# Splitting the 512-column matmuls of the weight-stationary units into matmuls of 256 columns

## The chip, the core and the metric

The kernel runs on one NeuronCore of a Trainium2 chip. The metric is the device time of one execution in microseconds (us), from before the first instruction to after the last. A profiled execution also gives the span from the first instruction to the last, and what each engine did in it: TensorE (PE in the profile, and PEld for its weight loads), VectorE (DVE), ScalarE (ACT), GpSimd (POOL), SyncE (SP) and the DMA queues.

## What is computed

One encoder layer on 256 positions of width 2048, in fp32. Cut to its matrix products, the reference is:

```python
h = rmsnorm(x, norm1_gain)
proj = h @ w_in                      # 2048 x 6144
o_d, o_l = diff_attention(...), dilated_window(...)     # on the columns of proj
x = x + concat([o_d, o_l]) @ w_out   # 2048 x 2048
h2 = rmsnorm(x, norm2_gain)
g, u = split(h2 @ w_gate_up)         # 2048 x 11264
g = depthwise_conv(g, conv_w, conv_b)
x = x + (silu(g) * u) @ w_down       # 5632 x 2048
return rmsnorm(x, final_gain)
```

## The kernel before, in words

**Products in three parts.** Each fp32 operand is split into a high part in the type fp32r and a low part that is the rest (`split`, L118: ScalarE writes the high part, VectorE subtracts to get the low part). A product then is high by high, plus high by low, plus low by high; low by low is left out. Activations lie as `hT`, `h2T`, `mT`, `aT`, each `[128, k tile, 2, 256]`: for each block of 128 rows of the contraction the 256 tokens' high parts (call them ah), and right behind them the 256 low parts (al). Weights come as raw tiles of 1 MB by DMA; each raw tile is split into two units of 1024 columns, `whi` and `wlo`.

**Units.** The list `units` (L157 to L190) is the order of all the work. A unit is 1024 weight columns, 512 KB, and `products` (L212) issues its matmuls; `mm` (L210) is the helper, so nearly all matmuls have line L210. There are two forms:

- Form A, with stationary activations: V columns, output projection, down projection. A unit is 12 matmuls of 512 columns, whose moving operand is a slice of `whi` or `wlo`.
- Form B, with stationary weights: query and key columns (`qk`, 16 groups of 4 units, on `hT`), and gate and up columns (`g` and `u`, 22 pairs of 256 columns each, 4 units each, on `h2T`). That is 64 and 176 units, 240 in all. A unit holds 4 k tiles by 256 output columns, that is 8 stationary tiles of 128x128 of each of `whi` and `wlo`. The 256 output columns are two column blocks, c = 0 and c = 1, each with a PSUM bank of its own: the accumulator `acc` is `[128, 2, 512]`.

In form B before, the first pass runs over the 8 `whi` tiles, and each multiplies all 512 columns of a k tile, ah and al at once. High by high so lands in the first 256 columns of the bank, high by low in the second 256. The second pass runs over the 8 `wlo` tiles with ah alone, 256 columns, into the first half:

```python
if p == 0:
    mm(P[:, c], w, a[:, kt], U["first"] and i == 0, False)
else:
    mm(P[:, c, :S], w, a[:, kt, 0], False, U["last"] and i == nk - 1)
```

**Reading an accumulator.** After the fourth unit of a group the two halves of each bank are added up (`sum_parts`, L337): ScalarE copies the second halves to SBUF (`half`, L340), VectorE adds them to the first (L341). `evac_qk` (L343) then scales the key block by the row of 1/rms (`R1`, L347), `gate` (L573) scales by `R2` (L578) and goes into the convolution, and `gated` (L598) multiplies by the activated gate (L603) and splits the result into `aT`. There are two accumulators, so that one is summed while the next group fills the other.

**Order around the change.** The loop at L675 goes unit by unit: it issues the DMA of raw tiles some units ahead on SyncE's queue, splits the weights of the unit three ahead (`AHEAD = 3`), issues the matmuls of this unit, and then whatever is tied to this unit's end (the dictionary `post`): attention steps, evacuations, gating. Each engine runs its instructions in that order. In the `qk` part the attention's small matmuls (scores L364 to L367, transposes L400 and L465, attention times V L421 to L425; tiles named `at`) stand between units.

Of the kernel before, what the change touches and what calls it, by code (L numbers as in the profile page):

```python
# [9 lines left out]
F32 = mybir.dt.float32  # L10
F32R = mybir.dt.float32r
BF16 = mybir.dt.bfloat16
AF = mybir.ActivationFunctionType
# [3 lines left out]
S = 256  # L17
# [32 lines left out]
def encoder_layer(ctx, tc, xT_d, x_d, w_d, sm_d, tab_d, fg_d, id_d, oh_d, lnc_d, out_d):  # L50
    nc = tc.nc
# [7 lines left out]
    att = att_stack.enter_context(tc.tile_pool(name="att", bufs=2))  # L59
    ctx.enter_context(tc.manual_schedule())  # L60

    def at_tile():
        return pat.tile([128, 512], F32, name="at", tag="at")
# [40 lines left out]
    p = at_tile()  # L104
# [13 lines left out]
    def split(hi, lo, src, gain=None):  # L118

        if gain is None:  # L120
            nc.scalar.activation(hi, src, AF.Copy)  # L121
            nc.vector.tensor_sub(lo, src, hi.bitcast(F32))  # L122
        else:
            nc.scalar.activation(hi, src, AF.Copy, scale=gain)  # L124
            nc.vector.scalar_tensor_tensor(lo, src, gain, hi.bitcast(F32),
                                           op0=ALU.mult, op1=ALU.subtract)
# [82 lines left out]
    def mm(out, lhsT, rhs, start, stop):  # L209
        nc.tensor.matmul(out, lhsT, rhs, start=start, stop=stop)  # L210

    def products(s, ts=(0, 1)):  # L212
        U = units[s]
        if U["first"]:
            if U["key"] == ("d", 3):
                accs[U["key"]] = [at_tile(), at_tile()]
            else:
                P = acc.tile([128, 2, 512], F32, name="acc", tag="acc")
                accs[U["key"]] = P if U["form"] == "B" else [P[:, 0], P[:, 1]]
        P = accs[U["key"]]  # L220
        a = A[U["act"]]()
        hi, lo = W[s]
        nk = len(U["kts"])
        if U["form"] == "A":
            wh, wl = (w.rearrange("p (k c) -> p k c", k=2) for w in (hi, lo))
            seq = []
            for i, t in ((i, t) for i in range(2) for t in ts):
                seq += [(i, t, 0, 0), (i, t, 0, 1), (i, t, 1, 0)]
            for t in ts:
                mine = [x for x in seq if x[1] == t]  # L230
                firsts, lasts = mine[0], mine[-1]
                seq = [x + ((x == firsts), (x == lasts)) if x[1] == t else x for x in seq]
            for i, t, x_, w_, f_, l_ in seq:
                mm(P[t], a[:, U["kts"][i], x_, t * 128:(t + 1) * 128], (wh, wl)[w_][:, i],
                   U["first"] and f_, U["last"] and l_)
        else:
            wh, wl = (w.rearrange("p (k c) -> p k c", k=4) for w in (hi, lo))

            seq = [(i, c, p) for p in range(2) for i in range(nk) for c in range(2)]
            for i, c, p in seq:  # L240
                kt = U["kts"][i]
                w = (wh, wl)[p][:, i, c * 128:(c + 1) * 128]

                if p == 0:
                    mm(P[:, c], w, a[:, kt], U["first"] and i == 0, False)
                else:
                    mm(P[:, c, :S], w, a[:, kt, 0], False, U["last"] and i == nk - 1)


    Z = dram.tile([NH, 128, 512], F32, name="Z")  # L250
# [19 lines left out]
    cst = {}  # L270
# [63 lines left out]

    G = defaultdict(dict)

    def sum_parts(pool, out, P):  # L337

        h = pool.tile([128, 2, S], F32, name="half", bufs=1)
        nc.scalar.activation(h, P[:, :, S:], AF.Copy)  # L340
        nc.vector.tensor_add(out, P[:, :, :S], h)  # L341

    def evac_qk(g):  # L343
        P = accs.pop(("qk", g))
        qk = att.tile([128, 2, S], F32, name="qk", bufs=1)
        sum_parts(att, qk, P)
        nc.vector.tensor_mul(qk[:, 1], qk[:, 1], cst["R1"])  # L347
        G[g]["qk"] = qk

    def split_qk(g):  # L350
# [140 lines left out]
    for g in range(16):  # L491
        e = end_slot["qk", g]
        first(e, evac_qk, g)
        first(e + 1, split_qk, g)
        at_slot(e + SC, scores, g)
        off = [SC, TR, AV, NO, MX]
        if g < 8:
            if g % 2 == 0:
                continue
            at_slot(e + SC + 1, diff_mix, g)  # L500
            e += 1
            for k in range(2, 5):
                off[k] += DD
        at_slot(e + TR, transp, g)
        for k, f in ((2, av), (3, norm_o), (4, mix_out)):
            at_slot(e + off[k], f, g)
# [52 lines left out]
    ml = {}  # L559
# [13 lines left out]
    def gate(pr):  # L573
        P = accs.pop(("g", pr))
        pool = ml["pool"]
        G2 = ml["gs"]
        sum_parts(pool, G2[:, :, 1:S + 1], P)
        nc.vector.tensor_mul(G2[:, :, 1:S + 1], G2[:, :, 1:S + 1],  # L578
                             cst["R2"][:, None, :].to_broadcast([128, 2, S]))
        y = pool.tile([128, 2, S], F32, name="y", bufs=1)  # L580
        ml["y"] = y
        for c in range(2):
            f = 2 * pr + c
            w = [sm[:, C_CW + 3 * f + i:C_CW + 3 * f + i + 1] for i in range(3)]
            gs = G2[:, c]
            nc.scalar.activation(y[:, c], gs[:, 1:S + 1], AF.Identity, bias=sm[:, C_CB + f:C_CB + f + 1],
                                 scale=w[1])
            nc.vector.scalar_tensor_tensor(y[:, c], gs[:, 0:S], w[0], y[:, c], op0=ALU.mult, op1=ALU.add)
            nc.vector.scalar_tensor_tensor(y[:, c], gs[:, 2:S + 2], w[2], y[:, c],
                                           op0=ALU.mult, op1=ALU.add)  # L590
# [7 lines left out]
    def gated(pr):  # L598
        P = accs.pop(("u", pr))
        aT = ml["aT"]  # L600
        a = ml["pool"].tile([128, 2, S], F32, name="a", bufs=1)
        sum_parts(ml["pool"], a, P)
        nc.vector.tensor_mul(a, a, ml.pop(("s", pr)))  # L603
        f = 2 * pr
        split(aT[:, f:f + 2, 0], aT[:, f:f + 2, 1], a)

    for pr in range(FT // 2):
        at_slot(end_slot["g", pr], gate, pr)
        at_slot(end_slot["g", pr] + 1, silu, pr)
        at_slot(end_slot["u", pr], gated, pr)  # L610
# [64 lines left out]
    for s in range(-AHEAD, NU):  # L675
        while n_loaded < NU // 2 and n_loaded * 2 <= s + AHEAD + 4:
            for _ in load_raw(n_loaded, 2 if n_loaded < 5 else 1):
                pass
            n_loaded += 1
            if X0 <= n_loaded < X0 + 4:  # L680
                load_x(n_loaded - X0)
        v = s + AHEAD
        if v < 8:
            split_unit(v, 2, lambda i: split_x(2 * v + i))
        elif v < NU:
            split_unit(v)
        if s == NU - AHEAD:
            break
        if s >= 0:
            products(s)  # L690
            del W[s]
            for f, a in post.pop(s, ()):
                f(*a)
    assert not post

    for t in range(2):
        for u in range(s, NU):
            products(u, (t,))
        final(t)
# [96 lines left out]
```

## Time and profile before

| what | value |
|---|---|
| device time, median of 3 runs | 1139.54 us (1139.11 to 1141.63) |
| device time of the profiled execution | 1139.58 us |
| its span | 1137.6 us |
| outside the span | 2.0 us |
| TensorE busy | 1125.6 us, 99% of the span, 6004 matmuls |
| weight loads busy | 962.0 us, 85%, 6004 loads |
| VectorE busy | 714.7 us, 63% |
| ScalarE busy | 577.7 us, 51% |
| DMA | 219.63 MB, mean 193 GB/s |

The busy time of TensorE is from the start of a matmul to its modelled end, and matmuls overlap; what a matmul costs in a dense stretch is the distance from its start to the start of the next one. A weight load overlaps the matmul before it. The time outside the span is the profiled execution's device time less its span.

### The profile page before, as it was taken

The page shows a single profiled execution, that of the slowest core. Times are in us where ns is not written, and L with a number is a line of the kernel's source. Part 1 is how long each engine was busy: PE and PEld are TensorE (multiplying, and loading weights), DVE is VectorE, ACT ScalarE, POOL GpSimd, SP SyncE. Part 2 cuts the span into 40 slices and gives each one's busy share as a digit, 9 for nine tenths or more (in the row PEclk, how much of TensorE's full clock was granted, in tenths as well). Part 3 has the DMA queues.
Part 4 walks back from the last instruction along what each step waited for, and adds up shares of the span by engine and source line. Part 5 has one row for each costly group of instructions (what it writes and reads, how often), then busy time and mean ns, then how long its engine had stood idle before and what let it go on. Part 6 is the DMA issues. An engine that isn't in the chain of part 4 may idle for free.

```text
span 1137.6 us, 14934 instructions
## 1 busy us (share of the span) xinstructions
PE 1125.6 (99%) x6004; PEld 962.0 (85%) x6004; DVE 714.7 (63%) x901; ACT 577.7 (51%) x814; POOL 22.0 (2%) x40
## 2 busy tenths in 40 slices
PE   8999999999999999999999999999999999999996
PEld 6878888888888888888888888888888888888885
DVE  7845667766655576676676667667666645454543
ACT  7544455666655555455454545545454434343432
POOL 0000000000000000000000000000000000000000
PEclk9999999999999999999999999999999999999999
DMA  9578445544444545454545455463645655555551
GB/s 333 195 256 321 161 179 179 182 163 167 173 160 177 190 183 191 179 192 179 222 153 218 181 188 187 184 221 149 222 173 198 228 205 197 185 190 196 204 186 74
DMA packets 34078, 219.63 MB, mean 193 GB/s; under 512 B 3905, under 2 KB 4289, under 8 KB 9433
## 3 DMA queue, kind: packets, MB, share of 16 engines
q1 hardware_dynamic: 31536, 211.17, 51.1%
q0 software_dynamic: 1776, 6.69, 1.6%
q8 instruction: 47, 0.77, 0.3%
q10 hardware_dynamic: 696, 0.81, 0.2%
q14 instruction: 23, 0.18, 0.0%
HBM read 216.54 MB, written 5.27 MB: 195 GB/s over the span
## 4 chain that ended last, share of the span: by engine, by line
PE 98%; DMA 0%; issue 0%; ACT 0%; DVE 0%; POOLq 0%; POOL 0%; DVEq 0%
PE acc L210 90%; PE at L210 7%; PE at L400 0%; DMA sm<-sm 0%; PE at L531 0%; PE at L465 0%; ACT jk L645 0%; POOLq L792 0%; PE at L255 0%; POOL r L651 0%; PE at L150 0%; DVEq L792 0%; ACT hT L124 0%; DVE x L657 0%; DVE x L643 0%
## 5 line engine op out<-in xcount | busy, mean ns | idle before, releaser
L122 DVE TENSOR_TENSOR wlo<-raw,whi 128x1024 fp32r<-128x1024 f32 (+1 forms) x400 | 471.4, 1200 | 220.6 <-ACT whi L121 220.4
L121 ACT ACTIVATE whi<-raw 128x1024 fp32r<-128x1024 f32 (+1 forms) x400 | 408.3, 1036 | 218.4 <-PE acc L210 176.0
L210 PE MATMUL acc<-h2T,whi 128*128 128x512 f32 x1408 | 356.5, 395 | 0.0
L210 PEld LDWEIGHTS acc<-h2T,whi 128*128 128x128 f32 x1408 | 251.7, 188 | 47.0
L210 PEld LDWEIGHTS acc<-h2T,wlo 128*128 128x128 f32 x1408 | 186.7, 188 | 16.0
L210 PE MATMUL acc<-h2T,wlo 128*128 128x256 f32 x1408 | 189.1, 277 | 0.0
L210 PE MATMUL acc<-whi,aT 128*128 128x512 f32 x528 | 162.8, 389 | 0.0
L210 PE MATMUL acc<-hT,whi 128*128 128x512 f32 x512 | 131.2, 398 | 0.0
L210 PEld LDWEIGHTS acc<-whi,aT 128*128 128x128 f32 x528 | 99.1, 188 | 20.7
L210 PEld LDWEIGHTS acc<-hT,whi 128*128 128x128 f32 x512 | 91.5, 188 | 17.5
L210 PE MATMUL acc<-wlo,aT 128*128 128x512 f32 x264 | 102.7, 389 | 0.0
L340 ACT ACTIVATE half<-acc 128x512 f32<-128x512 f32 x60 | 35.6, 593 | 118.2 <-PE acc L210 118.2
L210 PE MATMUL acc<-whi,hT 128*128 128x512 f32 x256 | 82.1, 399 | 1.9 <-ACT hT L124 1.9
L210 PE MATMUL acc<-whi,mT 128*128 128x512 f32 x256 | 82.7, 395 | 0.0
L210 PEld LDWEIGHTS acc<-hT,wlo 128*128 128x128 f32 x512 | 68.1, 188 | 5.9
L210 PE MATMUL acc<-hT,wlo 128*128 128x256 f32 x512 | 69.0, 277 | 0.0
L210 PEld LDWEIGHTS acc<-whi,hT 128*128 128x128 f32 x256 | 48.8, 191 | 14.2 <-ACT hT L124 2.8
L210 PEld LDWEIGHTS acc<-wlo,aT 128*128 128x128 f32 x264 | 49.6, 188 | 10.1
L210 PEld LDWEIGHTS acc<-whi,mT 128*128 128x128 f32 x256 | 48.1, 188 | 9.7
L210 PE MATMUL at<-whi,aT 128*128 128x512 f32 x176 | 54.4, 389 | 0.0
L210 PE MATMUL acc<-wlo,hT 128*128 128x512 f32 x128 | 50.5, 394 | 0.0
L210 PE MATMUL acc<-wlo,mT 128*128 128x512 f32 x128 | 49.9, 390 | 0.0
(123 smaller groups left out, 677.5 us busy)
## 6 DMA issues: line engine op xcount, KB each, us to landing
raw<-w SPq DMA_DIRECT2D x191, 1024.0 KB, 4.8
raw<-w SPq DMA_DIRECT2D x8, 512.0 KB, 7.5
Z<-Td POOLq DMA_DIRECT2D x1, 3072.0 KB, 19.6
Xb<-Z POOLq DMA_DIRECT2D x12, 192.0 KB, 4.2
x<-x SPq DMA_DIRECT2D x4, 512.0 KB, 11.6
xT<-xT SPq DMA_DIRECT2D x7, 256.0 KB, 7.1
raw<-w SPq DMA_DIRECT2D x4, 256.0 KB, 5.4
fg<-fg POOLq DMA_DIRECT2D x1, 1024.0 KB, 5.1
```

The costliest lines, as they stand in the source:

```text
L121: nc.scalar.activation(hi, src, AF.Copy)
L122: nc.vector.tensor_sub(lo, src, hi.bitcast(F32))
L210: nc.tensor.matmul(out, lhsT, rhs, start=start, stop=stop)
L340: nc.scalar.activation(h, P[:, :, S:], AF.Copy)
```

## The change

Form A keeps its matmuls and their order; its code is only written more simply. In form B a unit is now one matmul of 512 columns (the first `whi` tile of column block 0, with ah and al) and 22 of 256 columns: the other 7 `whi` tiles with ah, then the same 7 with al, then the 8 `wlo` tiles with ah. All 22 add into the first half of their bank. So each of those 7 `whi` tiles is stationary twice, in two passes. The columns that are multiplied stay the same: 8 x 512 + 8 x 256 = 6144 before, 512 + 22 x 256 = 6144 now. The second half of a bank is written for column block 0 alone, and so the halves are added up for that block alone (`sum_first`); block 1 is read from PSUM by the multiplication that follows.

```diff
@@ products, form B
-            seq = [(i, c, p) for p in range(2) for i in range(nk) for c in range(2)]
-            for i, c, p in seq:
-                kt = U["kts"][i]
-                w = (wh, wl)[p][:, i, c * 128:(c + 1) * 128]
-
-                if p == 0:
-                    mm(P[:, c], w, a[:, kt], U["first"] and i == 0, False)
-                else:
-                    mm(P[:, c, :S], w, a[:, kt, 0], False, U["last"] and i == nk - 1)
+            parts = ((wh, 0), (wh, 1), (wl, 0))
+            mm(P[:, 0], wh[:, 0, :128], a[:, U["kts"][0]], U["first"], False)
+            seq = [(i, c, j) for j in range(3) for i in range(nk) for c in range(2)]
+            seq = [x for x in seq if x not in ((0, 0, 0), (0, 0, 1))]
+            for i, c, j in seq:
+                w, x_ = parts[j]
+                mm(P[:, c, :S], w[:, i, c * 128:(c + 1) * 128], a[:, U["kts"][i], x_],
+                   U["first"] and (i, c, j) == (0, 1, 0), U["last"] and j == 2 and i == nk - 1)
@@
-    def sum_parts(pool, out, P):
-        h = pool.tile([128, 2, S], F32, name="half", bufs=1)
-        nc.scalar.activation(h, P[:, :, S:], AF.Copy)
-        nc.vector.tensor_add(out, P[:, :, :S], h)
+    def sum_first(pool, out, P):
+        h = pool.tile([128, S], F32, name="half", bufs=1)
+        nc.scalar.activation(h, P[:, 0, S:], AF.Copy)
+        nc.vector.tensor_add(out, P[:, 0, :S], h)
@@ evac_qk
-        sum_parts(att, qk, P)
-        nc.vector.tensor_mul(qk[:, 1], qk[:, 1], cst["R1"])
+        sum_first(att, qk[:, 0], P)
+        nc.vector.tensor_mul(qk[:, 1], P[:, 1, :S], cst["R1"])
@@ gate
-        sum_parts(pool, G2[:, :, 1:S + 1], P)
-        nc.vector.tensor_mul(G2[:, :, 1:S + 1], G2[:, :, 1:S + 1],
-                             cst["R2"][:, None, :].to_broadcast([128, 2, S]))
+        sum_first(pool, G2[:, 0, 1:S + 1], P)
+        nc.vector.tensor_mul(G2[:, 1, 1:S + 1], P[:, 1, :S], cst["R2"])
+        nc.vector.tensor_mul(G2[:, 0, 1:S + 1], G2[:, 0, 1:S + 1], cst["R2"])
@@ gated
-        sum_parts(ml["pool"], a, P)
-        nc.vector.tensor_mul(a, a, ml.pop(("s", pr)))
+        s = ml.pop(("s", pr))
+        sum_first(ml["pool"], a[:, 0], P)
+        nc.vector.tensor_mul(a[:, 1], P[:, 1, :S], s[:, 1])
+        nc.vector.tensor_mul(a[:, 0], a[:, 0], s[:, 0])
```

On TensorE, at the end of a group of `qk` units with the scores of an earlier group behind it, the order before is (each row is a matmul, its result, what it reads, its columns, and how many stand in a row):

```order
L210 MATMUL acc<-hT,whi 128x512 x8
L210 MATMUL acc<-hT,wlo 128x256 x8
L210 MATMUL at<-qks 128x256 x6
L210 MATMUL acc<-hT,whi 128x512 x8
L210 MATMUL acc<-hT,wlo 128x256 x8
```

and at the same place now:

```order
L210 MATMUL acc<-hT,whi 128x512
L210 MATMUL acc<-hT,whi 128x256 x14
L210 MATMUL acc<-hT,wlo 128x256 x8
L210 MATMUL at<-qks 128x256 x6
L210 MATMUL acc<-hT,whi 128x512
L210 MATMUL acc<-hT,whi 128x256 x14
```

Eight matmuls of 512 columns became one of 512 and fourteen of 256; what stands around them is where it was. The units on `h2T` read the same way.

On VectorE, at the first pair of the gate and up columns, from the reading of the gate accumulator (`gs`) to that of the up accumulator (`a`), the order before is:

```order
L341 TENSOR_TENSOR gs<-acc,half 128x2x256
L578 TENSOR_TENSOR gs<-gs,R_3803 128x2x256
L588 SCALAR_TENSOR_TENSOR y<-gs,sm,y 128x256
L589 SCALAR_TENSOR_TENSOR y<-gs,sm,y 128x256
L588 SCALAR_TENSOR_TENSOR y<-gs,sm,y 128x256
L589 SCALAR_TENSOR_TENSOR y<-gs,sm,y 128x256
L122 TENSOR_TENSOR wlo<-raw,whi 128x1024
L595 TENSOR_TENSOR y<-y,R_3803 128x512
L122 TENSOR_TENSOR wlo<-raw,whi 128x1024 x3
L341 TENSOR_TENSOR a<-acc,half 128x512
L603 TENSOR_TENSOR a<-a,y 128x512
```

and now:

```order
L339 TENSOR_TENSOR gs<-acc,half 128x256
L576 TENSOR_TENSOR gs<-acc,R_4279 128x256
L577 TENSOR_TENSOR gs<-gs,R_4279 128x256
L586 SCALAR_TENSOR_TENSOR y<-gs,sm,y 128x256
L587 SCALAR_TENSOR_TENSOR y<-gs,sm,y 128x256
L586 SCALAR_TENSOR_TENSOR y<-gs,sm,y 128x256
L587 SCALAR_TENSOR_TENSOR y<-gs,sm,y 128x256
L122 TENSOR_TENSOR wlo<-raw,whi 128x1024
L593 TENSOR_TENSOR y<-y,R_4279 128x512
L122 TENSOR_TENSOR wlo<-raw,whi 128x1024 x3
L339 TENSOR_TENSOR a<-acc,half 128x256
L602 TENSOR_TENSOR a<-acc,y 128x256
```

Two operations on 512 columns became three on 256 at each reading; nothing else changed its place.

## Rows read from the trace of the kernel before

**Rows 1.** The page: span, busy time by engine, granted clock in 40 slices, chain by engine.

```profile
span 1137.6 us, 14934 instructions
PE 1125.6 (99%) x6004; PEld 962.0 (85%) x6004; DVE 714.7 (63%) x901; ACT 577.7 (51%) x814; POOL 22.0 (2%) x40
PEclk9999999999999999999999999999999999999999
PE 98%; DMA 0%; issue 0%; ACT 0%; DVE 0%; POOLq 0%; POOL 0%; DVEq 0%
```

**Rows 2.** Waits of TensorE in the whole span: us in total, times, longest.

```profile
PE acc L210 <- ACT hT L124: 1.9, 1, 1.9
PE at L106 <- DVE warm L67: 1.2, 1, 1.2
```

**Rows 3.** Groups by form, TensorE: count | busy us, mean ns of one | idle before.

```profile
L210 PE MATMUL acc<-h2T,whi 128*128 128x512 f32 x1408 | 356.5, 395 | 0.0
L210 PEld LDWEIGHTS acc<-h2T,wlo 128*128 128x128 f32 x1408 | 186.7, 188 | 16.0
L210 PE MATMUL acc<-hT,whi 128*128 128x512 f32 x512 | 131.2, 398 | 0.0
```

**Rows 4.** Timeline of TensorE, eight and a half units on h2T: start us, us, what.

```profile
600.73 2.02 PE L210 MATMUL acc<-h2T,whi 128*128 128x512 f32 x8
602.59 1.07 PE L210 MATMUL acc<-h2T,wlo 128*128 128x256 f32 x8
603.50 2.02 PE L210 MATMUL acc<-h2T,whi 128*128 128x512 f32 x8
...
622.91 2.02 PE L210 MATMUL acc<-h2T,whi 128*128 128x512 f32 x8
```

**Rows 5.** Timeline inside that wlo run, from its second and its eighth matmul on.

```profile
602.71 0.39 PE L210 MATMUL acc<-h2T,wlo 128*128 128x256 f32 x2
...
603.39 0.28 PE L210 MATMUL acc<-h2T,wlo 128*128 128x256 f32 x1
```

**Rows 6.** Chain in order of time, qk part and end: start us, us, what, how many.

```profile
118.08 0.72 PE at L210 x6
118.80 11.11 PE acc L210 x64
154.02 2.13 PE at L210 x18
231.92 1.41 PE at L210 x12
240.03 0.89 PE at L210 x8
1068.85 55.77 PE at L210 x246
```

**Rows 7.** Groups by form: what reads an accumulator, and the nearest 256-column operations.

```profile
L340 ACT ACTIVATE half<-acc 128x512 f32<-128x512 f32 x60 | 35.6, 593 | 118.2 <-PE acc L210 118.2
L578 DVE TENSOR_TENSOR gs<-gs,R 128x512 f32<-128x512 f32 x22 | 15.2, 692 | 0.7
L341 DVE TENSOR_TENSOR gs<-acc,half 128x512 f32<-128x512 f32 x22 | 15.2, 691 | 41.5 <-ACT half L340 41.5
L124 ACT ACTIVATE h2T<-at,sm 128x256 fp32r<-128x256 f32 x16 | 7.4, 470 | 10.7 <-DVE h2T L125 8.1 <-PE at L531 2.5
L347 DVE TENSOR_TENSOR qk<-qk,R 128x256 f32<-128x256 f32 x16 | 6.8, 425 | 0.6
L643 DVE TENSOR_TENSOR x<-at,x 128x256 f32<-128x256 f32 x4 | 1.5, 420 | 4.6 <-PE at L210 4.5
```

**Rows 8.** One stretch of gate and up units: busy us by engine, clock, DMA share.

```profile
420.00:898.00 478.00, 478.00 (x2749) 416.17 (x2748) 327.02 (x387) 246.83 (x302) 0.58 (x1) 1.00 0.52 193
```

**Rows 9.** The page: the DMA queue that fetches instructions: packets, MB, share.

```profile
q8 instruction: 47, 0.77, 0.3%
```

More of the change, by code (lines that the diff above doesn't have):

```diff
@@ L225, in products @@
             wh, wl = (w.rearrange("p (k c) -> p k c", k=2) for w in (hi, lo))
-            seq = []
             for i, t in ((i, t) for i in range(2) for t in ts):
[L228 to L235, printed above, removed]
+                kt = U["kts"][i]
+                st, sp = U["first"] and i == 0, U["last"] and i == 1
+                ah = a[:, kt, 0, t * 128:(t + 1) * 128]
+                al = a[:, kt, 1, t * 128:(t + 1) * 128]
+                mm(P[t], ah, wh[:, i], st, False)
+                mm(P[t], ah, wl[:, i], False, False)
+                mm(P[t], al, wh[:, i], False, sp)
         else:
             wh, wl = (w.rearrange("p (k c) -> p k c", k=4) for w in (hi, lo))
-            seq = [(i, c, p) for p in range(2) for i in range(nk) for c in range(2)]
-            for i, c, p in seq:
-                kt = U["kts"][i]
-                w = (wh, wl)[p][:, i, c * 128:(c + 1) * 128]
-                if p == 0:
-                    mm(P[:, c], w, a[:, kt], U["first"] and i == 0, False)
-                else:
-                    mm(P[:, c, :S], w, a[:, kt, 0], False, U["last"] and i == nk - 1)
+            parts = ((wh, 0), (wh, 1), (wl, 0))
[6 more added lines that the diff above has]
+                   U["first"] and (i, c, j) == (0, 1, 0), U["last"] and j == 2 and i == nk - 1)
     Z = dram.tile([NH, 128, 512], F32, name="Z")
```

## The prediction

> **What bounds the kernel now.** The page comes first: TensorE is busy for 99% of the span, the granted clock is full in every slice, and the chain that ends last is TensorE for 98% [rows 1]. The waits of TensorE say whether it is held up by anybody: two waits in the whole run, 3.1 us together [rows 2]. So the time is the sum of the distances from each matmul's start to the next one's, and a change helps or hurts by what it does to that distance. The mean duration of a matmul is no such price: 395 ns for 512 columns [rows 3], where eight of them take 1.86 us.
>
> The distances are read from the timeline. Between 600.73 and 622.91 us stand eight whole units on `h2T`, so one takes 22.18 / 8 = 2.7725 us [rows 4]. Inside it the eight matmuls of 512 columns take 602.59 back to 600.73 = 1.86 us, 0.2325 us each, and the eight of 256 take 0.91 us. A finer cut of that second run [rows 5] has its second start at 602.71 and its eighth at 603.39: the first distance, straight behind the 512s, is 0.12 us, and the next six are 0.68 / 6 = 0.1133 us. A unit on `hT` takes 11.11 / 4 = 2.7775 us, from the piece of 64 matmuls [rows 6].
>
> **What stands out:** twice 0.1133 is 0.2267, less than 0.2325. In form B 512 columns at once cost 5.9 ns more than two matmuls of 256. In the down projection they don't: its last 246 matmuls of 512 columns take 55.77 us, 0.2267 each [rows 6], just twice 0.1133.
>
> **The change, part by part.**
>
> *Matmuls.* The counts 1408 and 512 over 8 in a unit [rows 3] give 176 units on `h2T` and 64 on `hT`. Each loses seven matmuls of 512 columns and gains fourteen of 256, each with a weight load. The nearest row for the fourteen is the run in rows 5: the same moving tile (seven of them even the same ah columns), the same alternation between the two banks, the same shape of stationary tile, `whi` for `wlo`. The other seven move al, which no 256-column row shows. I take 0.1133 for all, and keep the extra of the first one behind a 512:
>
> - after: 0.2325 + 0.12 + 21 x 0.1133 = 2.7325 us a unit
> - saved: 176 x (2.7725 - 2.7325) + 64 x (2.7775 - 2.7325) = 7.0 + 2.9 = 9.9 us
>
> The ends of this case: with 0.2267 for the 512 and 0.1133 for all 22 a unit takes 2.7193, and 13.1 us are saved; with the whole run's mean, 0.9125 / 8 = 0.1141, for all 22 it takes 2.7427, and 7.5 us are saved.
>
> *Weight loads.* A load's record lasts 188 ns [rows 3], longer than 0.1133, but eight of them in 0.91 us already overlap, and six distances in a row are even; loads that fell behind would stretch the later ones. So no separate price, except in a rival below.
>
> *Clock.* It reads 1.00, the 2.4 GHz level, in a stretch of 478 us of such units [rows 8]. TensorE gets no pause that it didn't have, so no change.
>
> *Splits and loads of weights.* They have to keep up with a unit that is 1.5% shorter. VectorE is busy 327 of 478 us there, ScalarE 247, the DMA engines 52% [rows 8]: hidden. The first `wlo` matmul comes 0.04 us earlier in its unit, against a lead of three units.
>
> *Reading an accumulator.* On ScalarE one copy shrinks from 593 ns towards the 470 of a 256-column read from PSUM; on VectorE 691 + 692 become three of about 420 to 425 [rows 7], some 0.1 us less. The accumulator's last read moves from 0.59 + 0.69 = 1.28 us behind the group's end to about 0.47 + 2 x 0.42 = 1.31. Its next user comes a whole group, 11 us, later. Cost nothing; if that cover went, 0.03 us for each of 60 groups, 2 us.
>
> *Instruction fetch.* 1680 more matmuls with as many loads, on top of 14934 instructions, for a queue that takes 0.3% of the DMA engines [rows 9]. Nothing, unless it lands late; no wait on it shows now.
>
> **The sum:** 1139.58 - 9.9 = 1129.7 us. The profiled execution (2.0 us outside its span) is within 0.1 us of the median, so no correction.
>
> **The rivals.**
>
> *Same: the price lies in al.* If the 5.9 ns belong to the low half of the columns and not to the length, al costs 0.2325 - 0.1133 = 0.1192 alone: a unit is 0.2325 + 0.12 + 14 x 0.1133 + 7 x 0.1192 = 2.773, and the time 1139.4 us. For it: no row has al alone, and 512-column matmuls on other tiles don't pay. Against it: al lies 1 KB further in the same tile, and nothing in the matmul knows which half it reads.
>
> *Slower: a long run doesn't hold the pace of a short one.* Eight matmuls behind eight long ones may live on what was issued ahead; 22 in every unit can't. From 0.1155 us a matmul on ((2.7725 - 0.2325) / 22) the change loses, only 2 ns above 0.1133. For it: the longer runs of 256 columns in the attention, which stand straight behind eight `wlo` matmuls, go slower: 2.13 / 18 = 0.1183, 1.41 / 12 = 0.1175, 0.72 / 6 = 0.12 us [rows 6]. At 0.1183 a unit takes 2.835 and the time is 1154.3; at 0.1175 it is 1150.1, at 0.12 1163.3. Against it: those are slow from their first matmul on and add into one bank three times over, and the piece of eight 128-column matmuls goes at 0.89 / 8 = 0.111 us behind eight `wlo` too [rows 6], sixteen pairs of load and matmul without a slowdown.
>
> *Slower by less: each matmul carries a fixed piece.* Then the fourteen cost half of a 512 plus that piece. By rows it lies between nothing and 0.12 - 0.1163 = 3.7 ns, which gives 1139.4 to 1152 us, 1145.7 in the middle. For it: the `qks` rows. Against it: twice 0.1133 equals the 0.2267 of the down projection, a piece of zero. The Trainium skill, "TensorE: Matmul & The Clock Gate", section "Back-to-back issue gap", states this rule: N / 2.4 ns plus 2.5 ns a matmul. By it seven more matmuls in 240 units would cost 7 x 240 x 2.5 ns = 4.2 us, about 1143.8, an estimate. The trace disagrees on this kernel: by that formula 256 columns are dearer per column than 512, and in form B they are cheaper.
>
> That the matmuls don't change as written is no case: the order on TensorE shows one, fourteen and eight.
>
> **How the numbers follow.** The forecast stands on a row of the same tile, banks and shape: 0.62, with a range of its own of 1126.5 to 1132.1. Price in al: 0.14. Long runs slower: 0.15. Fixed piece: 0.09. A measurement of this kernel can tell about 0.2%, 2.3 us. Faster by more than that: the forecast and a sliver of the al case, 0.63. Within: most of the al case and the low end of the fixed piece, 0.15. Slower: the rest, 0.22. The range reaches from 1126.5 over the al case into the fixed piece, to 1146: 0.62 + 0.14 + 0.05 = 0.81; the long runs are left out above.
>
> **What would show it.** Right: in the changed profile's timeline a unit on `h2T` takes 2.72 to 2.74 us, its fourteen `whi` matmuls follow each other at 0.113 to 0.114 us, ah and al alike, TensorE still has no wait, and the `half` copies shrink. Wrong: the second seven slower than the first (al), distances that grow along the run or lie near 0.118 throughout (long runs), one even distance of 0.116 to 0.12 (a fixed piece), or new waits of TensorE.

## The result and the profile after

The change made the kernel slower: 1150.62 us (1150.15 to 1151.32) against 1139.53 us of the kernel before on the same chip, 1.0094 times, 95% interval 1.0077 to 1.0112. That is 11.1 us longer, where 9.9 us shorter was forecast. The time lies outside the range, which ended at 1146.0; the rival of the long runs had been given 1150.1 for a distance of 0.1175 us.

The page of the changed kernel, the lines that answer to [rows 1]:

```profile
span 1148.7 us, 18338 instructions
PE 1136.1 (99%) x7684; PEld 1046.2 (91%) x7684; DVE 700.1 (61%) x945; ACT 565.2 (49%) x814; POOL 22.0 (2%) x40
PEclk9999999999999999999999999999999999999998
```

TensorE is still busy for 99% and holds 1680 matmuls more; the queue that fetches instructions still takes 0.3% of the DMA engines. Its waits, for [rows 2]:

```profile
PE acc L210 <- ACT hT L124: 2.1, 2, 1.7
PE at L106 <- DVE warm L67: 1.2, 1, 1.2
```

So no new wait: 3.3 us in all instead of 3.1. The 11 us lie in the distances between matmuls. The timeline of TensorE in the changed kernel, eight units on `h2T`, for [rows 4] (start us, us, what; the view merges a unit's one matmul of 512 columns with the fourteen of 256 behind it, and names the run by its first):

```profile
600.35 2.05 PE L210 MATMUL acc<-h2T,whi 128*128 128x512 f32 x15
602.23 1.10 PE L210 MATMUL acc<-h2T,wlo 128*128 128x256 f32 x8
603.17 2.05 PE L210 MATMUL acc<-h2T,whi 128*128 128x512 f32 x15
...
622.96 2.05 PE L210 MATMUL acc<-h2T,whi 128*128 128x512 f32 x15
```

A unit takes 22.61 / 8 = 2.826 us, 0.054 more than before. The eight `wlo` matmuls, which the change did not touch, take 0.94 us instead of 0.91: 0.1175 each instead of 0.114. So the same matmuls on the same tiles became slower, and it isn't the fourteen new ones alone. By this difference 176 units would make 176 x 0.0537 = 9.5 us. Taken in the two timelines from the first unit to the end of the last, the gate and up part grew from 489.4 to 498.6 us, by 9.2, and the `qk` part from 205.9 to 207.3 us, by 1.4.

In the `qk` part the changed kernel's own timeline shows something that no price of a matmul explains, four units on `hT` behind the scores:

```profile
119.24 2.05 PE L210 MATMUL acc<-hT,whi 128*128 128x512 f32 x15
121.13 1.11 PE L210 MATMUL acc<-hT,wlo 128*128 128x256 f32 x8
122.07 1.98 PE L210 MATMUL acc<-hT,whi 128*128 128x512 f32 x15
123.89 1.07 PE L210 MATMUL acc<-hT,wlo 128*128 128x256 f32 x8
124.80 2.04 PE L210 MATMUL acc<-hT,whi 128*128 128x512 f32 x15
126.67 1.10 PE L210 MATMUL acc<-hT,wlo 128*128 128x256 f32 x8
127.62 2.05 PE L210 MATMUL acc<-hT,whi 128*128 128x512 f32 x15
```

From start to start the units take 2.83, 2.73 and 2.82 us. One unit ran at the forecast's length (2.7325 us), its `wlo` run in 0.91 us, and the next one, the same 23 matmuls, fell back. Of the 240 units 18 have such a fast `wlo` run, 16 of them in the `qk` part, and a slow one follows each time.

The other engines behave as forecast. The stretch of [rows 8], now (busy us of PE, PEld, DVE, ACT, POOL, then the clock and the DMA share), and the copy of [rows 7]:

```profile
420.00:898.00 478.00, 478.00 (x3892) 470.16 (x3891) 313.16 (x424) 234.71 (x297) 0.00 (x0) 1.00 0.52 187
```

```profile
L338 ACT ACTIVATE half<-acc 128x256 f32<-128x256 f32 x60 | 22.6, 377 | 122.1 <-PE acc L210 122.1
```

The clock reads 1.00 in the slow stretch as it did before, VectorE and ScalarE have less to do than in [rows 8], and the copy fell from 593 to 377 ns, below the 470 that was assumed.

### The profile page after: what moved, and what is told of

Its sections match the earlier page's. It is cut to its first block, busy times and chain, and to the rows that moved or that the text cites. A ratio compares the mean times of both kernels' runs of the same rounds, so it can differ in the third digit from the quotient of the medians.

```text
span 1148.7 us, 18338 instructions
## 1 busy us (share of the span) xinstructions
PE 1136.1 (99%) x7684; PEld 1046.2 (91%) x7684; DVE 700.1 (61%) x945; ACT 565.2 (49%) x814; POOL 22.0 (2%) x40
## 4 chain that ended last, share of the span: by engine, by line
PE 98%; DMA 1%; issue 0%; ACT 0%; DVE 0%; POOLq 0%; POOL 0%; DVEq 0%
PE acc L210 89%; PE at L210 7%; DMA raw<-w 1%; PE at L398 0%; PE at L463 0%; PE at L529 0%; ACT jk L645 0%; POOLq L792 0%; PE at L253 0%; POOL r L651 0%; PE at L150 0%; DVEq L792 0%; ACT whi L121 0%; DVE x L657 0%; DVE x L643 0%
## 5 line engine op out<-in xcount | busy, mean ns | idle before, releaser
L210 PE MATMUL acc<-h2T,whi 128*128 128x256 f32 (+1 forms) x2640 | 360.5, 289 | 0.0
L210 PEld LDWEIGHTS acc<-h2T,whi 128*128 128x128 f32 x2640 | 336.6, 189 | 8.3
L210 PE MATMUL acc<-h2T,wlo 128*128 128x256 f32 x1408 | 194.4, 281 | 0.0
L210 PEld LDWEIGHTS acc<-h2T,wlo 128*128 128x128 f32 x1408 | 178.0, 189 | 0.0
L210 PE MATMUL acc<-hT,whi 128*128 128x256 f32 (+1 forms) x960 | 131.5, 289 | 0.0
L210 PEld LDWEIGHTS acc<-hT,whi 128*128 128x128 f32 x960 | 121.5, 189 | 3.0
L338 ACT ACTIVATE half<-acc 128x256 f32<-128x256 f32 x60 | 22.6, 377 | 122.1 <-PE acc L210 122.1
L210 PEld LDWEIGHTS acc<-hT,wlo 128*128 128x128 f32 x512 | 64.3, 189 | 0.0
```

What stands on the lines that cost most here:

```text
L338: nc.scalar.activation(h, P[:, 0, S:], AF.Copy)
```

## The experiments

Three theories stood at the start. **F:** each matmul carries a fixed piece beside its columns. **L:** only long runs of 256-column matmuls are slow. **E:** the reading of the accumulators has a part. Behind the first batch came **S:** the stream of matmuls has two paces that keep themselves up, 0.1133 and 0.1177 us per 256 columns, and what comes ahead decides which.

### Reading the accumulators alone

```diff
-            parts = ((wh, 0), (wh, 1), (wl, 0))
...
+            seq = [(i, c, p) for p in range(2) for i in range(nk) for c in range(2)]
...
     def sum_first(pool, out, P):
```

The matmuls of before, with the new `sum_first` and its three users kept.

> The matmuls of before with the change's way of reading the accumulators; the high by low product of column block 1 is computed and never added. Theories F and L: TensorE's rows do not change, 1139.5 us within 2 us. Rival: the new reading costs something by itself; then part of the 11 us shows here.

Measured: 1139.54 us against 1139.65, ratio 0.9999 (0.9990 to 1.0009). E falls: the way of reading costs nothing by itself, and the 11 us are TensorE's.

### Twenty matmuls, in short runs

The `whi` pass is now this, with the `wlo` pass behind it as it was:

```diff
...
+            for i in range(nk):
+                kt = U["kts"][i]
+                w0, w1 = wh[:, i, :128], wh[:, i, 128:]
+                mm(P[:, 0], w0, a[:, kt], U["first"] and i == 0, False)
+                mm(P[:, 1, :S], w1, a[:, kt, 0], U["first"] and i == 0, False)
+                mm(P[:, 1, :S], w1, a[:, kt, 1], False, False)
...
```

> Form B units with four matmuls of 512 columns (column block 0) and sixteen of 256: per k tile 512, 256, 256, so that no run of 256-column matmuls is longer than before's eight, save that the last two join the wlo run; 20 matmuls a unit instead of 16 (before) and 23 (the change). Theory F, a fixed piece per matmul beside its columns: the unit is 2.560 us (6144 columns at 2.4 per ns) + 20 x 11.6 to 13.3 ns = 2.792 to 2.827 us, the time 1144 to 1152 us. Theory L, only long runs of 256 are slow and short ones cost 0.1133 each: the unit is 4 x 0.2325 + 16 x 0.1133 + 0.01 = 2.753 us, the time about 1135 us.

Measured: 1140.69 us, ratio 1.0009 (1.0000 to 1.0018). The timeline of this kernel:

```profile
602.25 2.03 PE L210 MATMUL acc<-h2T,whi 128*128 128x512 f32 x12
604.11 1.07 PE L210 MATMUL acc<-h2T,wlo 128*128 128x256 f32 x8
605.02 2.03 PE L210 MATMUL acc<-h2T,whi 128*128 128x512 f32 x12
```

A unit takes 2.77 us with 20 matmuls, as with 16. That is below the 2.792 that F wants at least, and it isn't L's 2.753 either.

### The sixteen matmuls of before, alternating

```diff
-            seq = [(i, c, p) for p in range(2) for i in range(nk) for c in range(2)]
+            seq = [(i, c, p) for i in range(nk) for c in range(2) for p in range(2)]
```

> The matmuls of before, 8 of 512 columns and 8 of 256, in another order: each whi tile is followed by its wlo tile, so 512 and 256 alternate. Theory F: the number of matmuls decides, the unit stays at 2.773 us and the time at 1139.5 us within 2 us, whatever the distances between starts show. Theory L: no run of 256 is left, each stands behind a 512 at 0.12 us, the 512s stay at 0.2325, so the unit is 2.82 us and the time about 1151 us; or, if a 256 keeps 0.1133 and each 512 falls to the 0.2267 of the down projection, 2.72 us and 1127 us.

Measured: 1151.86 us, ratio 1.0109 (1.0092 to 1.0126). One pair after the other in its timeline:

```profile
599.82 0.40 PE L210 MATMUL acc<-h2T,whi 128*128 128x512 f32 x1
600.05 0.28 PE L210 MATMUL acc<-h2T,wlo 128*128 128x256 f32 x1
600.17 0.40 PE L210 MATMUL acc<-h2T,whi 128*128 128x512 f32 x1
...
602.64 0.40 PE L210 MATMUL acc<-h2T,whi 128*128 128x512 f32 x1
```

Eight pairs take 2.82 us: the very matmuls of before, no more of them, and as slow as the change. F falls here, since the number did not change. L's first number, 1151, is met, but for a kernel without any long run.

### All twenty-four of 256 columns

```diff
-            mm(P[:, 0], wh[:, 0, :128], a[:, U["kts"][0]], U["first"], False)
-            seq = [x for x in seq if x not in ((0, 0, 0), (0, 0, 1))]
...
-        sum_first(pool, G2[:, 0, 1:S + 1], P)
+        nc.vector.tensor_mul(G2[:, 0, 1:S + 1], P[:, 0, :S], cst["R2"])
```

> All 24 matmuls of a form B unit have 256 columns, and no halves are added up at all: the accumulators are read once by the operation that follows. Theory F: one matmul more than the change, 8 to 13 ns a unit, 2 to 3 us above it, so 1152.5 to 1154 us. Theory L: 24 x 0.1175 = 2.820 us, 0.007 below the change's unit, about 1149 us. If the reading of the accumulators has a part in the 11 us, this one loses that part and comes out below 1148.

Measured: 1146.20 us, ratio 1.0057 (1.0042 to 1.0072), below both numbers. It is below E's 1148 as well, but the timeline gives another reason: in most of the `qk` part a unit takes 2.72 us, in the gate and up part 2.83 us, with the same 24 matmuls. The gate and up part takes 498.8 us, against 498.6 in the changed kernel; the `qk` part takes 202.8 instead of 207.3.

```profile
132.93 1.98 PE L210 MATMUL acc<-hT,whi 128*128 128x256 f32 x16
134.74 1.07 PE L210 MATMUL acc<-hT,wlo 128*128 128x256 f32 x8
135.65 1.07 PE L210 MATMUL acc<-hT,whi 128*128 128x256 f32 x8
...
601.79 2.05 PE L210 MATMUL acc<-h2T,whi 128*128 128x256 f32 x16
603.68 1.11 PE L210 MATMUL acc<-h2T,wlo 128*128 128x256 f32 x8
604.62 2.05 PE L210 MATMUL acc<-h2T,whi 128*128 128x256 f32 x16
```

2.72 / 24 = 0.1133, held without any 512 for units on end: L falls, and so does the rival that al is dearer, for a third of these matmuls move al. Left were S, and the chance that something in the gate and up part itself is slow (R below).

### Foreign matmuls between the units

A small group whose result nobody reads, behind every second gate accumulator; once on the kernel with 24 matmuls, once on the change.

```diff
+    def kick(kind, n):
+        h2, p = A["t"], at_tile()
+        for i in range(n):
+            if kind == "K":
+                mm(p[:, :S], h2[:, 0, int(i % 3 == 2), :128], h2[:, 1, int(i % 3 == 1)], True, True)
+            elif kind == "M":
+                mm(p, h2[:, 0, 0, :128], h2[:, 1], True, True)
+            else:
+                nc.tensor.transpose(out=p[:, :128], in_=ident, identity=ident)
...
```

> All 24 matmuls of form B have 256 columns (as in e3_all_256, whose units took 2.720 us in most of the qk part and 2.827 us in all of the gate and up part), and in the gate and up part a small foreign group of matmuls, whose result nobody reads, stands behind every second gate accumulator: 6 of 256 columns from one tile into one bank, 4 transposes, one 512, six again, one 256, 2 transposes, six, two 512s, three 256s, 4 transposes, six; some 4 us of added work. Theory S: the stream of matmuls has paces that keep themselves up (0.1133 and 0.1177 us per 256 columns), which one it takes is decided by what stood ahead, and a foreign group can switch it; some stretches between the groups then run at 2.720 us a unit and others at 2.827, even within each. Theory R: the gate and up part is slow because of what runs beside it or of its tile; all its units stay at 2.827 and the time is about 1150 us.

Measured: 1146.84 us in one run, against 1140.12 of the kernel before beside it. Its timeline, at the first transposes and at the second group of six:

```profile
477.49 1.11 PE L210 MATMUL acc<-h2T,wlo 128*128 128x256 f32 x8
478.43 0.60 PE L610 MATMUL at<-ident 128*128 128x128 f32 x4
478.79 2.08 PE L210 MATMUL acc<-h2T,whi 128*128 128x256 f32 x16
480.70 1.07 PE L210 MATMUL acc<-h2T,wlo 128*128 128x256 f32 x8
481.61 1.98 PE L210 MATMUL acc<-h2T,whi 128*128 128x256 f32 x16
...
565.27 1.07 PE L210 MATMUL acc<-h2T,wlo 128*128 128x256 f32 x8
566.18 0.88 PE L210 MATMUL at<-h2T 128*128 128x256 f32 x6
566.89 2.05 PE L210 MATMUL acc<-h2T,whi 128*128 128x256 f32 x16
568.78 1.10 PE L210 MATMUL acc<-h2T,wlo 128*128 128x256 f32 x8
```

Four transposes turn a stream whose `wlo` run takes 0.94 us into one of 0.91, and it stays so for 87 us, over a lone 512 at 522 us; six matmuls turn it back. In the same kernel two 512s in a row switched slow to fast, three 256s fast to slow, one 512 left a fast stream fast, and the other groups left a slow one slow, the second set of transposes among them. Gate and up units run at 2.72 as well as at 2.83: R falls, S holds.

> The change (one 512, 22 of 256 a unit) with the same foreign groups. Theory S with the lone 512 as what keeps the slow pace up: every unit meets a 512 again, so after each foreign group the units come back to 2.827 us, and the time is that of the change plus about 4 us, 1154 to 1155. If the 512 does nothing, stretches at about 2.725 us appear as in the other kernel.

Measured: 1155.77 us in one run beside 1140.12, a little above the 1154 to 1155 that were expected. On the change the units come back to 2.826 us within two units of every group. Behind the four transposes at 482.60 us, the first set, which made the other kernel fast:

```profile
484.93 1.10 PE L210 MATMUL acc<-h2T,wlo 128*128 128x256 f32 x8
485.87 2.05 PE L210 MATMUL acc<-h2T,whi 128*128 128x512 f32 x15
```

The `wlo` run still takes 0.94 us. The reading that S gives is that the lone 512 of each unit throws the stream back, as behind the unit at 122.07 us in the changed kernel itself; the kernel without that 512, below, bears it out.

### Two 512s in a unit

The lines are shown against the change:

```diff
-            mm(P[:, 0], wh[:, 0, :128], a[:, U["kts"][0]], U["first"], False)
+            for c in range(2):
+                mm(P[:, c], wh[:, 0, c * 128:(c + 1) * 128], a[:, U["kts"][0]], U["first"], False)
...
```

The rest is the kernel before, so the halves are added up for both blocks.

> The change with two matmuls of 512 columns at the head of each form B unit (both column blocks' first whi tile) and 20 of 256, and the halves added up for both blocks as before. Theory S: what matters is the state that the 512s leave, not their number; two 512s in a row switched the slow stream to the fast one in the kernel with foreign groups, so units of 2.72 to 2.77 us can come out (1127 to 1140 us); if two do the same as one, 2.827 us and 1150 us. A fixed price for each matmul would lie between 16 and 23 matmuls, at 22: 2.819 us and 1149 us.

Measured: **1130.57 us**, ratio 0.9920 (0.9906 to 0.9935), faster than both kernels. Its timeline:

```profile
603.76 1.99 PE L210 MATMUL acc<-h2T,whi 128*128 128x512 f32 x14
605.59 1.07 PE L210 MATMUL acc<-h2T,wlo 128*128 128x256 f32 x8
606.49 1.99 PE L210 MATMUL acc<-h2T,whi 128*128 128x512 f32 x14
```

2.73 us a unit with 22 matmuls: one more 512 than the change, and 20 us less. The fixed price's 1149 us are far off.

### Three 512s in a unit

Against the kernel with two:

```diff
-            for c in range(2):
-                mm(P[:, c], wh[:, 0, c * 128:(c + 1) * 128], a[:, U["kts"][0]], U["first"], False)
+            for i, c in ((0, 0), (0, 1), (1, 0)):
+                mm(P[:, c], wh[:, i, c * 128:(c + 1) * 128], a[:, U["kts"][i]], U["first"] and i == 0, False)
...
```

> Form B units with three matmuls of 512 columns at the head and 18 of 256; the halves are added up for both blocks. Theory S with the 512s as switches: in the changed kernel a single 512 took a fast stream to the slow pace, two in a row leave it fast (unit of 2.733 us); then three leave it slow: unit 2.827 us, 1150 to 1152 us. If only a 512 standing alone does it, three in a row leave it fast: 3 x 0.2333 + 18 x 0.1133 = 2.740 us, 1132 us.

Measured: 1140.31 us, ratio 1.0007 (0.9997 to 1.0016), neither number. The timeline shows both at once:

```profile
600.46 2.03 PE L210 MATMUL acc<-h2T,whi 128*128 128x512 f32 x13
602.33 1.11 PE L210 MATMUL acc<-h2T,wlo 128*128 128x256 f32 x8
603.27 2.00 PE L210 MATMUL acc<-h2T,whi 128*128 128x512 f32 x13
605.11 1.07 PE L210 MATMUL acc<-h2T,wlo 128*128 128x256 f32 x8
606.01 2.03 PE L210 MATMUL acc<-h2T,whi 128*128 128x512 f32 x13
```

Units of 2.81 and 2.74 us take turns, all through the part: each group of three 512s turns the pace over, from fast to slow and from slow to fast. So S holds with the 512s as switches, and the expectation was wrong in holding that three always end slow.

### A foreign group once

On the kernel with 24 matmuls of 256 columns; the second kernel has `(("T", 4))` in the place of `(("M", 2))`.

```diff
+    for pr, (kind, n) in ((0, ("M", 2)),):
+        at_slot(end_slot["g", pr], kick, kind, n)
```

> All 24 matmuls of form B have 256 columns, and two foreign matmuls of 512 columns, whose result nobody reads, stand once, behind the first gate accumulator. Theory S, and if they switch the stream as they did once: 172 units at 2.720 instead of 2.827 us, 18 us less than without them, 1128 us. If the switch depends on where in the stream they fall, 1146.5 us as without them.

Measured with two 512s: 1147.18 us, ratio 1.0066 (1.0051 to 1.0081): the stream is not switched, at another place than where two had done it.

> The same with four foreign transposes instead. They switched the stream in one of two places. Theory S: 1128 us if they switch it, 1146.5 us if not. Nothing in between, since a stream that has a pace keeps it.

Measured with four transposes: **1128.50 us**, ratio 0.9902 (0.9886 to 0.9919), the fastest full computation here. The view by stretches of this kernel, to be set beside the slow stretch above (PE, PEld, DVE, ACT, POOL busy, clock, DMA share):

```profile
420.00:860.00 440.00, 440.00 (x3885) 440.00 (x3884) 285.32 (x365) 209.86 (x243) 0.00 (x0) 1.00 0.54 193
```

The clock is the same 1.00. Nothing between the two numbers came out, as S says: four useless transposes of 0.4 us save 17.7 us against the kernel that is otherwise the same, and 18.7 us against the one with two 512s at the very same place.

### The change without its one 512, and the same bank twice in a row

Both on the kernel of the last experiment, with its four transposes. The first runs the order of the change, with the first matmul cut to 256 columns:

```diff
-            for i, c, j in [(i, c, j) for j in range(3) for i in range(nk) for c in range(2)]:
+            for i, c, j in [(i, c, j) for j in range(3) for i in range(nk) for c in range(2) if (i, c, j) != (0, 0, 1)]:
```

> The order of the change, 23 matmuls a unit with one break in the alternation of the two banks, but its first matmul has 256 columns instead of 512 (the high by low product of that one tile is left out of the computation), and four foreign transposes stand once behind the first gate accumulator. Theory S1, the lone 512 holds the slow pace: without it the fast pace can hold, 23 x 0.1133 = 2.607 us a unit behind the transposes. Theory S2, the odd number of matmuls or the repeated bank holds it: 23 x 0.1178 = 2.709 us throughout, and the time 18 us longer than by S1.

Measured: 1101.04 us in one run; it also computes a little less. Its timeline, at the start of the gate and up part:

```profile
395.94 1.86 PE L210 MATMUL acc<-h2T,whi 128*128 128x256 f32 x15
397.64 1.07 PE L210 MATMUL acc<-h2T,wlo 128*128 128x256 f32 x8
398.55 1.86 PE L210 MATMUL acc<-h2T,whi 128*128 128x256 f32 x15
...
401.59 0.60 PE L610 MATMUL at<-ident 128*128 128x128 f32 x4
```

2.61 us a unit, 0.113 a matmul, in the order of the change with its odd count and its repeated bank: S1. The units run so ahead of the four foreign transposes at 401.59 us, so these have no part in it, other than was expected. In the `qk` part, which no foreign group precedes, all 64 `wlo` runs go at 0.113 us a matmul, against 16 of 64 in the changed kernel; on TensorE the two differ there in the length of each unit's first matmul alone. So it is the lone 512 that holds the stream at the slow pace. Taking its second 256 columns away takes 0.22 us from the unit (2.826 to 2.61), nearly twice what they cost.

The second uses each `whi` tile for the high and straight after it for the low columns:

```diff
-            for i, c, j in [(i, c, j) for j in range(3) for i in range(nk) for c in range(2)]:
+            for i, c, j in [(i, c, j) for i in range(nk) for c in range(2) for j in range(2)] + [(i, c, 2) for i in range(nk) for c in range(2)]:
```

> All 24 matmuls of form B have 256 columns, with the transposes once as in k5, but each whi tile is used for the high and straight after it for the low columns, so that the same bank and the same stationary tile come twice in a row. S1: bank and tile do not matter, the fast pace of 2.720 us a unit is possible as in k5 (1128.5 us), or the slow one at 2.827 us if the transposes do not switch this stream (1146). S2 with the repeated bank as the cause: every unit has eight repeats and none runs at 2.720.

Measured: 1129.21 us in one run. Behind the transposes a unit takes 2.72 us: a bank and a tile that come twice in a row don't keep a stream from the fast pace.

## Why the prediction was wrong

- **That TensorE sets the time, and nothing else moves.** Right: no new wait, the clock at 1.00, the reading of the accumulators worth nothing by itself (ratio 0.9999).
- **"The nearest row for the fourteen is the run in rows 5", and 0.1133 for all 22.** This is the step that failed. The run's six even distances were taken for a price of these matmuls. They were the pace of the stream in that stretch, and the changed unit doesn't keep it: 0.1175 in the `wlo` run, which is the row itself, made slower by what stands ahead of it. That the row would keep its own value was doubted only by the rival of the long runs, and of the single matmuls the signs named for "right" take the fourteen `whi` alone, not the row.
- **The arithmetic behind it.** Right where the pace is held: 2.7325 us a unit was worked out, and the changed kernel's own unit at 122.07 us has it. The kernel with two 512s, another kernel than the forecast's, has 2.73 and 1130.57 us, where 1129.7 was forecast.
- **The rival of the long runs.** Its number came true (1150.1 for 0.1175; 1150.62), and so did its sign, distances near 0.118 throughout. Its mechanism did not, so the number is luck: runs without end hold 0.1133 in the kernels with 24 matmuls, and short ones go slow in the alternating order. The attention's pieces that it stood on, 0.1175 to 0.12 in [rows 6], are not the slow pace either. The 256-column matmuls of attention times V stand 0.1175 us apart on average in the kernel before, in the one with two 512s and in the one with four transposes, and every `wlo` run of the `qk` part goes at 0.113 to 0.115 there. The prediction was right to set these pieces aside; no run shows why they are slower.
- **The rival of al.** Wrong: al goes at 0.1133 in the fast units with 24 matmuls.
- **The fixed piece.** Wrong: 20 matmuls take the time of 16, 24 take 11.2 us less than 16 did once the stream is fast, and the same 24 matmuls take 2.72 or 2.83 us. The Trainium skill's N / 2.4 plus 2.5 ns ("TensorE: Matmul & The Clock Gate", section "Back-to-back issue gap"), which it gives there for an isolated matmul, would make each added matmul cost something if it were taken as a price in a stream. No run agrees with that.
- **That 512 columns cost more than twice 256 in form B.** Half right. In the kernel before the 0.2325 is neither the one pace (0.2267) nor the other (twice 0.1175) but a mean of unlike distances: in the trace of a gate and up unit the eight 512s take 0.226, then 0.236 and 0.231 by turns, and 0.236 is twice 0.118. So the slow pace could be seen in the kernel before, in the 512s and in the first distance behind them (0.12 in [rows 5]), which was kept as an extra of one matmul.

Not settled: what in the engine holds a pace, and why one and the same group switches it at one place and not at another. Even a lone 512 is not of one kind: straight behind a slow unit of the changed kernel it leaves the stream slow nearly always and turned it fast six times, as at 122.07 us, and a foreign one left a fast stream of 24 matmuls a unit fast. The runs show the switch and its effect, not the mechanism.

## What to carry to other kernels

The distance between two matmuls in a dense stretch belongs to the stretch, not to the matmul: before it is used as a price in another order, look in the same trace at the single distances of the same stream, and take a disagreement of some per cent (here 0.226, 0.236 and 0.231 us for eight equal matmuls in a row) as the range, not as something to average away. If a change of order costs or gives a few per cent on a TensorE that has no waits, compare a run of matmuls that the change did not touch, before and after; if it moved as well, try other groupings of the long and the short matmuls, or a small group of foreign ones, before the change is dropped.

## What was not expected of the hardware

- One and the same stream of 256-column matmuls in fp32r, with a new stationary tile each, runs at 0.1133 or at 0.1178 us a matmul and keeps that for 87 us in one kernel and for 468 us, to the end of the part, in another; in both the granted clock reads 1.00, the 2.4 GHz level.
- Four transposes, or two matmuls of 512 columns, can switch it up; six or three of 256 switched it down. The same group did so at one place and not at another. The times repeat from run to run: 1146.17 to 1146.41 us in four runs of the kernel with 24 matmuls, 1127.97 to 1128.83 in four with the transposes.
- At the head of a unit of else 256-column matmuls, one 512 holds the slow pace (2.826 us a unit), two in a row the fast one (2.73), and three turn it over in every unit (2.81 and 2.74).
